# An attention layer on one core: attention and the first output quarter in the order of a list schedule, zero key halves from DRAM

## The chip, the core and the metric

The kernel runs on one core of a Trainium2 chip. The core has TensorE (PE) for matmuls, VectorE (DVE), ScalarE (ACT) and GpSimd (POOL) for elementwise work, and SyncE (SP), which issues most DMA transfers. Each engine takes its instructions from a queue of its own, in order, and waits on semaphores for what others must have done. The metric is device time in microseconds (us); lower is better. "Granted clock" is the share of TensorE's full clock that the profiler records.

## What is computed

One layer of a diffusion backbone on 512 latent tokens and 256 context tokens, width 2048, in float32. Both streams are normalised and modulated, projected, and go through two kinds of attention, eight heads of each, whose outputs are concatenated and projected by `w_o`. A gated MLP with a convolution follows. The part that the change touches, cut from the reference:

```python
def _diff_attend(q, k, v, lam):                       # 8 heads, two halves of 64 channels
    s1 = einsum('bhqd,bhkd->bhqk', q1, k1) * DA_SCALE
    s2 = einsum('bhqd,bhkd->bhqk', q2, k2) * DA_SCALE
    w = softmax(s1) - lam * softmax(s2)
    return einsum('bhqk,bhkd->bhqd', w, v)
def _softmax_attend(q, k, v, scale):                  # 8 latent heads, 128 + 64 channels
    return einsum('bhqk,bhkd->bhqd', softmax(einsum('bhqd,bhkd->bhqk', q, k) * scale), v)
o_da = _rmsnorm(o_da, subln_w) * (1.0 - lambda_init)  # per head
x = x + g1 * (concat(o_da, o_mla) @ w_o)
```

Queries are the 512 latent tokens, keys and values are all 768. Latent heads get queries, keys and values from small latents (`c_q`, `c_kv`) by a second projection; queries and keys of the latent tokens are rotated.

## The kernel before

A float32 product runs on TensorE as three matmuls of a faster 32-bit type: each operand is split into a high part (a cast, on ScalarE) and a low part (the rest, on VectorE), and `mm3` adds high by high, high by low and low by high. `split` and `wblock` make such pairs (lines 80, 81 and 104 to 106 in the profile); a weight block is a load `wr`, then `wh` and `wl`, with three buffers of each.

The stages around the change, in time:

- The projections of keys and values end with the values of heads 4 to 7: six tiles of PSUM are split into `kh` and `kl` (two buffers each) and stored to DRAM (`v_d`) by GpSimd.
- Eight differential heads (`da_head`). For each: the projection of the head's queries (`feature`, tile `f`, 16 steps of three matmuls), rotation and scaling into `qs`; keys `ks` (both parts stacked) and `klz` (low parts beside zeros) come from DRAM. For each quarter of 128 queries and each half: scores into a PSUM tile `s` of two buffers, a row maximum on VectorE, an exponential with its sum on ScalarE (line 514). GpSimd scales the second half (567), VectorE combines both (568). `weighted_values` then, for six blocks of 128 keys: four transposes into `pt`, a split into `wth` and `wtl`, and the product with the values into `po`. The output goes to DRAM (`o_d`).
- Eight latent heads, in pairs. `latent_pair` makes queries, keys and values of two heads; then scores of five matmuls, softmax, transposes, products. `sub_norm` normalises one differential head's output beside each latent head: a square, its sum over channels by a matmul with ones in plain float32 (653), four passes of VectorE.
- The output projection in four quarters of 64 steps of three matmuls each; the first three are in a loop (`for g in range(3)`), with passes over the modulation weights (`gemv`) from the second on.

The order of each engine's instructions comes from a scheduler that fills the queues by program order and priority; nothing is written by hand in this stretch. PSUM has, beside the two `s` buffers, four tiles here: one `pt`, two `f`, one `po`. The zero halves of `klz` and `krlz` are set by GpSimd with memsets.

```python
    for h in range(NH):
        da_head(h, da_queries(h))
    ap_.release()
...
        if i == 0 and h + 2 < NH:
            nxt = latent_pair(h // 2 + 1)
        sub_norm(h)
        oraw[8 + h] = b2k()
        weighted_values(mb, ws, lambda kt: [v[:, i * P:(i + 1) * P] for v in vs[kt]], oraw[8 + h], h == NH - 1)
```

Of the kernel before, what the change touches and what calls it, by code (L numbers as in the profile page):

```python
# [9 lines left out]
F32 = mybir.dt.float32  # L10
F32R = mybir.dt.float32r
# [37 lines left out]
NSMALL = _o  # L49


@with_exitstack
def layer_kernel(ctx: ExitStack, tc: tile.TileContext, small, rope, c_row, cc_row, x_t, ctx_t, ada, ada_k,
# [72 lines left out]
    ones32 = cst.tile([P, P], F32, name="ones32")  # L126
# [379 lines left out]
    def scores_softmax(mms, pool, tag, bufs, l):  # L506
        s = s_tile()
        for c0, c1 in ((0, T), (T, TT)):
            for i, (a, b) in enumerate(mms):
                pe.matmul(s[:, c0:c1], a, b[:, c0:c1], start=i == 0, stop=i == len(mms) - 1)  # L510
        m = sm.tile([P, 1], F32, tag="m", name=nm("m"), bufs=4)
        ve.tensor_reduce(out=m, in_=s[:, :TT], axis=AX.X, op=ALU.max, negate=True)
        p = pool.tile([P, TT], F32, tag=tag, name=nm(tag), bufs=bufs)
        sc.activation(p, s[:, :TT], AF.Exp, bias=m, accum_out=l)
        return p

    def weighted_values(pool, ws, v, dst, last=False):
        po = b_tile("po", 1)
        for kt in range(NKEY):
            pt = b_tile("f", 2) if last and kt % 3 else b_tile("pt", 1)  # L520
            for qt in range(NQT):
                pe.transpose(pt[:, qt * P:(qt + 1) * P], ws[qt][:, kt * P:(kt + 1) * P], ident)
            wth, wtl = split_tiles(pool, ("wth", "wtl"), [P, T], 2, pt)
            mm3(po, v(kt), (wth, wtl), kt == 0, kt == NKEY - 1)
        sc.copy(dst, po)
# [10 lines left out]
    def da_rtmp():  # L536
        return da.tile([P, T], F32, tag="rt", name=nm("rt"), bufs=2)

    def da_queries(h):
        if h == 0:  # L540
            qs = [da.tile([P, T], F32R, tag=f"qs{i}", name=nm("qs"), bufs=2) for i in range(2)]
            for i in range(2):
                nc.sync.dma_start(qs[i].bitcast(F32), q0_d[i])
            return qs
        lat = b_tile("f", 2)
        feature(lat, None)
        q = da_rtmp()
        apply_rope(q, lat, da_rtmp)
        return stacked_queries(da, q, DA_SCALE)

    def da_head(h, qs):
        ks = da.tile([P, 2, TT], F32R, tag="ks", name=nm("ks"), bufs=2)
        kl = klz[h % 2]
        for i, r in enumerate((lo, hi)):
            nc.sync.dma_start(ks[r].bitcast(F32), k_d[h][0].rearrange("(i p) n -> p i n", i=2))
            nc.sync.dma_start(kl[r, i].bitcast(F32), k_d[h][1][r])
        v = da.tile([P, 2, NKEY, P], F32R, tag="v", name=nm("v"), bufs=2)
        nc.sync.dma_start(v.bitcast(F32), v_d[h // 4][h % 4])
        ws = []
        for qt in range(NQT):  # L560
            c = slice(qt * P, (qt + 1) * P)
            l = sm.tile([P, 2], F32, tag="l", name=nm("l"), bufs=4)
            ps = [scores_softmax([(qs[i][:, c], ks[:, i]), (qs[i][:, c], kl[:, i])], da, f"p{i}", (8, 3)[i],
# [9 lines left out]

    for h in range(NH):
        da_head(h, da_queries(h))
    ap_.release()


    mc = tc.alloc_tile_pool(name="mc", bufs=1, side="right", reuse_waits="tile")
# [834 lines left out]
```

## Time and profile before

| | us |
|---|---|
| median of 3 runs (2439.32 to 2442.99) | 2439.42 |
| span of the profiled execution | 2439.6 |
| TensorE busy | 2367.0 |
| VectorE busy | 1735.5 |
| ScalarE busy | 1117.0 |
| GpSimd busy | 220.2 |

The profile is of one execution. A row of a timeline gives the start, the duration, the engine, the line, the operation and what it writes and reads; in brackets stands how long the engine sat idle before it and what ended that. A row of a group gives the count, the busy time and the mean in nanoseconds, then the idle time ahead of the group and its releasers. A wait row gives the total, the number of times and the longest. Where a shape is 128x512, a tile has 128 partitions and 512 elements in each.

### The profile page before, as it was taken

To read this page: it belongs to the slowest core of one execution; us is meant where nothing else is said; L and a number is where in the kernel's file an instruction comes from. 1 tells how busy PE (TensorE), PEld (TensorE's weight loads), DVE (VectorE), ACT (ScalarE), POOL (GpSimd) and SP (SyncE) were. 2 spreads that over 40 slices of the span, in tenths; PEclk is the share of its full clock that TensorE was granted. 3 is DMA by queue.
4 is the path that set the end of the run, shared out by engine and by line. 5 is a ranking of instruction groups with operands and counts; after the bars stand their busy time and mean duration, and the time that the engine had idled before them with its cause. 6 is when DMAs were issued, how large, how long until landed. Compare 5 with 4: busy or idle time off the path is not lost.

```text
span 2439.6 us, 32889 instructions
## 1 busy us (share of the span) xinstructions
PE 2367.0 (97%) x12758; PEld 1978.4 (81%) x12758; DVE 1735.5 (71%) x2316; ACT 1117.0 (46%) x1696; POOL 220.2 (9%) x244
## 2 busy tenths in 40 slices
PE   6999999999999999999999999999999999999998
PEld 3678877777777778889888888888888888888888
DVE  6668876388868878378667676767666666666667
ACT  4432121155646542245445454545454545454545
POOL 0000000121100003100111111111111111111110
PEclk9999999999999999999999999999999999999999
DMA  8758889555411149423555555555555565556573
GB/s 300 279 211 309 327 319 330 181 166 144 127 59 44 44 161 349 146 87 113 147 130 143 134 140 137 137 139 136 141 134 143 132 143 132 141 135 140 133 188 111
DMA packets 130707, 403.32 MB, mean 165 GB/s; under 512 B 14323, under 2 KB 25075, under 8 KB 122099
## 3 DMA queue, kind: packets, MB, share of 16 engines
q1 hardware_dynamic: 104118, 350.87, 43.7%
q0 software_dynamic: 25280, 49.30, 11.6%
q8 instruction: 100, 1.64, 0.3%
q10 hardware_dynamic: 1152, 1.05, 0.1%
q14 instruction: 57, 0.47, 0.1%
HBM read 331.68 MB, written 69.48 MB: 164 GB/s over the span
## 4 chain that ended last, share of the span: by engine, by line
PE 76%; DVE 8%; issue 7%; ACT 4%; DMA 3%; POOL 2%; SPq 0%; DVEq 0%; ACTq 0%; POOLq 0%
PE y L1133 11%; PE b L105 9%; PE b L104 9%; PE b L106 9%; PE z L1133 5%; PE y L1135 5%; PE s L104 3%; PE s L105 3%; PE s L106 3%; PE z L1135 3%; PE s L510 3%; PE x L1133 2%; DMA ada<-in_ada 2%; PE b L206 1%; PE f L104 1%
## 5 line engine op out<-in xcount | busy, mean ns | idle before, releaser
L989 DVE TENSOR_TENSOR wl<-wr,wh 128x1024 fp32r<-128x1024 f32 x144 | 176.4, 1225 | 157.8 <-ACT wh L981 157.1
L981 ACT CAST wh<-wr 128x1024 fp32r<-128x1024 f32 x144 | 151.0, 1049 | 234.0 <-PE b L105 118.5
L104 PE MATMUL b<-ah,wh 128*128 128x512 f32 (+1 forms) x664 | 256.8, 387 | 0.0
L105 PE MATMUL b<-al,wh 128*128 128x512 f32 (+1 forms) x664 | 256.7, 387 | 0.0
L106 PE MATMUL b<-ah,wl 128*128 128x512 f32 (+1 forms) x664 | 255.9, 385 | 0.0
L1154 POOL DMA_DIRECT2D x_d<-xs x160 | 139.6, 1004 | 1162.6 <-ACT xs L1153 1159.3
L989 DVE TENSOR_TENSOR wl<-rb,wh 128x1024 fp32r<-128x1024 f32 x123 | 150.0, 1220 | 126.9 <-ACT wh L981 126.8
L981 ACT CAST wh<-rb 128x1024 fp32r<-128x1024 f32 x123 | 129.2, 1050 | 185.7 <-PE b L105 116.1
L989 DVE TENSOR_TENSOR wl<-ws,wh 128x1024 fp32r<-128x1024 f32 x123 | 150.1, 1220 | 90.1 <-ACT wh L981 90.1
L80 ACT CAST wh<-wr 128x1024 fp32r<-128x1024 f32 (+3 forms) x102 | 99.2, 972 | 217.0 <-PE b L106 62.1
L171 DVE CUSTOM_DVE_ANT_0 ada<-ada,cb,smt 128x2048 f32<-128x2048 f32 x64 | 152.5, 2382 | 54.6 <-DMA ada<-in_ada 54.2
L981 ACT CAST wh<-ws 128x1024 fp32r<-128x1024 f32 x123 | 128.2, 1043 | 130.3 <-DVE ws L943 44.3
L1133 PE MATMUL y<-a2k,wh 128*128 128x512 f32 x656 | 164.0, 392 | 0.0
L81 DVE TENSOR_TENSOR wl<-wr,wh 128x1024 fp32r<-128x1024 f32 (+3 forms) x102 | 116.9, 1146 | 62.1 <-ACT wh L80 61.7
L104 PE MATMUL b<-a2k,wh 128*128 128x512 f32 (+1 forms) x376 | 141.6, 377 | 5.9 <-ACT a2k L838 4.3
L106 PEld LDWEIGHTS b<-ah,wl 128*128 128x128 f32 x664 | 124.8, 188 | 25.7
L104 PEld LDWEIGHTS b<-ah,wh 128*128 128x128 f32 x664 | 125.1, 188 | 22.9
L105 PEld LDWEIGHTS b<-al,wh 128*128 128x128 f32 x664 | 125.1, 188 | 21.9
L105 PE MATMUL b<-a2k,wh 128*128 128x512 f32 (+1 forms) x376 | 140.8, 374 | 0.0
L106 PE MATMUL b<-a2k,wl 128*128 128x512 f32 (+1 forms) x376 | 140.0, 372 | 0.0
L1133 PEld LDWEIGHTS y<-a2k,wh 128*128 128x128 f32 x656 | 118.6, 189 | 21.6
L1133 PE MATMUL y<-b2k,wh 128*128 128x512 f32 x410 | 107.8, 393 | 0.0
(454 smaller groups left out, 5757.2 us busy)
## 6 DMA issues: line engine op xcount, KB each, us to landing
ada<-in_ada SPq DMA_DIRECT2D x64, 1024.0 KB, 6.4
rb<-in_w_up SPq DMA_DIRECT2D x123, 512.0 KB, 4.3
wr<-in_w_dn SPq DMA_DIRECT2D x88, 512.0 KB, 4.3
x_d<-xs POOLq DMA_DIRECT2D x160, 256.0 KB, 6.0
wr<-in_w_up SPq DMA_DIRECT2D x53, 512.0 KB, 4.2
wr<-in_w_f SPq DMA_DIRECT2D x34, 512.0 KB, 6.0
ada<-in_ada SPq DMA_DIRECT2D x32, 512.0 KB, 6.4
adak<-in_ada_k SPq DMA_DIRECT2D x32, 512.0 KB, 6.3
```

Of the source, the lines that this page charges most:

```text
L80: sc.copy(dst_h, src)
L81: ve.tensor_tensor(dst_l, src, dst_h.bitcast(F32), op=ALU.subtract)
L104: pe.matmul(out, st[0], mv[0], start=start, stop=False, **kw)
L105: pe.matmul(out, st[0], mv[1], start=False, stop=False, **kw)
L106: pe.matmul(out, st[1], mv[0], start=False, stop=stop, **kw)
L171: ve.tensor_tensor_reduce(out=junk, in0=w, in1=vec, op0=ALU.mult, op1=ALU.add, scale=1.0, scalar=col("b_ada", j), accum_out=dst[:, j:j + 1])
L510: pe.matmul(s[:, c0:c1], a, b[:, c0:c1], start=i == 0, stop=i == len(mms) - 1)
L981: sc.copy(t, raw[:, k * n_:k * n_ + n_])
L989: ve.tensor_tensor(t, raw[:, k * n_:k * n_ + n_], hi[k].bitcast(F32), op=ALU.subtract)
L1133: pe.matmul(o, w[j][0], hs[j], start=start and j == 0, stop=False, skip_group_check=True)
L1135: pe.matmul(o[:, h0], w[j][1], hs[j][:, h0], start=False, stop=j == 7, skip_group_check=True)
L1154: gp.dma_start(x1_d[dt], x, accum_op=ALU.add)
```

## The change

Attention of both kinds and the first output quarter are no longer issued in the program's order. Each piece of work becomes a step with an engine, a cost, a due time `at`, and the buffers that it reads and writes. `Flow.run` goes through these steps as a list schedule: on each of five engines the open step with the least due time is taken, as far as its inputs are ready by the costs and a buffer of its ring is free. The instructions are then issued in that order, and the scheduler keeps it on all five engines. Due times come from a table of spans for the sixteen heads.

The work itself changes in these places:

- The zero halves of `klz` are loaded by SyncE from a block of zeros in DRAM, which GpSimd writes at the kernel's start from a zeroed tile. The latent heads' zero halves use the same tile.
- The combination of the two softmax maps: VectorE's pass over 768 columns is replaced by a scaling on ScalarE and a sum on GpSimd (behind GpSimd's scaling, which stays).
- `sub_norm`: the square is split in two parts, and its sum takes two matmuls of the faster type; VectorE's four passes and the final scaling go to GpSimd (six passes) and ScalarE.
- PSUM: two `pt`, one `f`, one `po`; four of a pair's six value blocks are projected into the unused columns of an `s` tile.
- Values of a latent pair share the buffers of the differential heads' values.
- The first output quarter's steps, and the splits of the sixteen head outputs that it reads, are in the same schedule; its gemv passes stay in the second and third quarters.

```diff
+class Flow:
+    LAGS = {"PE": 0.25, "ACT": 0.07, "DVE": 0.07, "POOL": 0.1, "SP": 3.5, "X": 0.0}
...
+            for e in engines:
+                while engines[e] <= now + 1e-9:
+                    can = [s for s in open_[e] if s.ready <= now + 1e-9 and all(free(b) for b in s.takes)]
+                    if not can:
+                        break
+                    s = min(can, key=lambda s: (s.at, s.n))
...
+                    engines[e] = now + s.cost
+                    order.append(s)
...
+        for s in order:
+            s.fn()
...
+    zero_d = dram.tile([64, TT], F32, name="zero_d")
...
+    for c0, c1, r in ((0, 480, slice(0, 64)), (480, TT, slice(64, P))):
+        gp.dma_start(zero_d[:, c0:c1].rearrange("p (k j) -> p k j", j=(c1 - c0) // KT),
+                     cpad[r, :, 2:2 + (c1 - c0) // KT])
...
-    def weighted_values(pool, ws, v, dst, last=False):
-        po = b_tile("po", 1)
+    def weighted_values(t, pace, ws, v, vr, dst, after=None):
+        po = buf(lambda: b_tile("po", 1), "po", 1)
         for kt in range(NKEY):
-            pt = b_tile("f", 2) if last and kt % 3 else b_tile("pt", 1)
...
+            pt = buf(lambda: b_tile("pt", 2), "pt", 2)
...
+            step("PE", 0.44, t0, turn, r=ws, w=[pt])
+            parts(t0 + 0.6, wt, pt, lambda b: b(), lambda pt=pt: pt())
+            step("PE", 0.69, t0 + 2.5, lambda wt=wt, kt=kt: mm3(po(), v(kt), [b() for b in wt], kt == 0,
+                                                                 kt == NKEY - 1), r=[*wt, *vr(kt)], w=[po])
...
+    SPANS = [17, 23.2, 23.2, 23.2, 23.2, 23.2, 23.2, 19] + [21, 22.8, 21, 22.8, 21, 22.8, 21, 16]
...
-    klz = [da.tile([P, 2, TT], F32R, name=nm("klz")) for _ in range(2)]
-    for t in klz:
-        for i, r in enumerate((hi, lo)):
-            gp.memset(t[r, i].bitcast(F32), 0.0)
+    for n_, (t, b) in enumerate(zip(klz, zeroed)):
+        for i, r in enumerate((hi, lo)):
+            step("SP", 0.1, FIRST + 3 * n_, lambda t=t, i=i, r=r: nc.sync.dma_start(t[r, i].bitcast(F32), zero_d), w=[b])
...
-            gp.tensor_scalar(out=ps[1], in0=ps[1], scalar1=rl[:, 1:2], scalar2=neglam, op0=ALU.mult, op1=ALU.mult)
-            ve.scalar_tensor_tensor(out=ps[0], in0=ps[0], scalar=rl[:, 0:1], in1=ps[1], op0=ALU.mult, op1=ALU.add)
+            step("POOL", 1.15, t + 0.2, lambda p=ps[1], rl=rl: gp.tensor_scalar(
+                out=p(), in0=p(), scalar1=rl()[:, 1:2], scalar2=neglam, op0=ALU.mult, op1=ALU.mult), r=[rl], w=[ps[1]])
+            step("ACT", 0.95, t + 0.2, lambda p=ps[0], rl=rl: sc.mul(p(), p(), rl()[:, 0:1]), r=[rl], w=[ps[0]])
+            step("POOL", 1.9, t + 1.5, lambda ps=ps: gp.tensor_tensor(out=ps[0](), in0=ps[0](), in1=ps[1](),
+                                                                      op=ALU.add), r=[ps[1]], w=[ps[0]])
...
-        pe.matmul(po, ones32, q, start=True, stop=True)
-        rstd(rs, po, P, mb.tile([P, T], F32, tag="sq", name=nm("s1"), bufs=1), t2)
+        step("ACT", 0.6, t + 4.4, lambda: sc.copy(qh(), q()), r=[q], w=[qh])
+        step("POOL", 1.3, t + 5, lambda: gp.tensor_tensor(out=ql(), in0=q(), in1=qh().bitcast(F32), op=ALU.subtract),
+             r=[q, qh], w=[ql])
+        step("PE", 0.46, t + 7, lambda: [pe.matmul(f(), onesr, g(), start=i == 0, stop=i == 1)
+                                         for i, g in enumerate((qh, ql))], r=[qh, ql], w=[f])
...
+    for kb in range(8):
+        t = tw + 8 * 0.9 * kb
+        w = block(t, w_o[0, kb])
...
+    with tc.manual_schedule(engines={mybir.EngineType.PE, mybir.EngineType.Activation, mybir.EngineType.DVE,
+                                     mybir.EngineType.SP, mybir.EngineType.Pool}):
+        flow.run()
```

**The start of the first differential head.** SyncE's queue before, behind the last value weights; `wr` are weight blocks of later query projections, `qs` and `ks` the first head's queries and keys:

```order
L90 DMA wr_3757<-in_w_f 128x1024
L90 DMA wr_4043<-in_w_f 128x1024
L90 DMA wr_4049<-in_w_f 128x1024
L90 DMA wr_4291<-in_w_f 128x1024
L90 DMA wr_4297<-in_w_f 128x1024
L543 DMA qs_3815<-q_d 128x512
L543 DMA qs_3816<-q_d 128x512
L555 DMA ks_3819<-k_d_128 64x2x768
```

The same place after:

```order
L215 DMA wr_3760<-in_w_f 128x1024
L755 DMA klz_3817<-zero_d 64x768
L765 DMA qs_3824<-q_d 128x512
L765 DMA qs_3826<-q_d 128x512
L755 DMA klz_3818<-zero_d 64x768
L755 DMA klz_3817<-zero_d 64x768
L755 DMA klz_3818<-zero_d 64x768
L773 DMA ks_3831<-k_d_128 64x2x768
```

Four weight blocks that stood ahead of the first queries and keys now stand behind them, and four loads of zeros are added. On VectorE, where `kl` are the low parts of the last values and `m` the row maxima of the scores, before:

```order
L81 TENSOR_TENSOR wl_4046<-wr_4043,wh_4045 128x1024
L81 TENSOR_TENSOR kl_3776<-s_3394,kh_3775 128x512
L81 TENSOR_TENSOR kl_3782<-s_3394,kh_3781 128x512
L81 TENSOR_TENSOR kl_3788<-b_3395,kh_3787 128x512
L81 TENSOR_TENSOR kl_3794<-b_3396,kh_3793 128x512
L81 TENSOR_TENSOR wl_4052<-wr_4049,wh_4051 128x1024
L512 TENSOR_REDUCE m_3832<-s_3827 128x1
```

and after:

```order
L206 TENSOR_TENSOR kl_3773<-s_3396,kh_3772 128x512
L206 TENSOR_TENSOR kl_3779<-s_3397,kh_3778 128x512
L206 TENSOR_TENSOR kl_3785<-s_3397,kh_3784 128x512
L206 TENSOR_TENSOR kl_3791<-b_3398,kh_3790 128x512
L206 TENSOR_TENSOR kl_3797<-b_3399,kh_3796 128x512
L698 TENSOR_REDUCE m_3859<-s_3851 128x1
L698 TENSOR_REDUCE m_3889<-s_3879 128x1
```

The splits of weight blocks between the value splits are gone from here; the value splits still stand ahead of the first maximum.

**The weights of a differential head.** TensorE before, where the second head's first transposes (`pt` from the weights `p` of its four quarters) stand among the third head's scores (`s`), the first head's last product (`po`) and a query projection (`f`):

```order
L106 MATMUL po_3919<-wth_3985,v_3824 128x512
L522 MATMUL pt_4168<-ident,p_4082 128x128
L522 MATMUL pt_4168<-ident,p_4105 128x128
L522 MATMUL pt_4168<-ident,p_4128 128x128
L510 MATMUL s_4346<-klz_3809,qs_4309 128x512
L510 MATMUL s_4346<-ks_4315,qs_4309 128x256
L510 MATMUL s_4346<-klz_3809,qs_4309 128x256
L104 MATMUL f_4490<-a2k_1556,wh_4299 128x512
L105 MATMUL f_4490<-a2k_1557,wh_4299 128x512
L106 MATMUL f_4490<-a2k_1556,wl_4300 128x512
L522 MATMUL pt_4168<-ident,p_4151 128x128
```

and after, at the third head's first transposes:

```order
L695 MATMUL s_4600<-ks_4272,qs_4506 128x512
L695 MATMUL s_4600<-klz_3818,qs_4506 128x512
L695 MATMUL s_4600<-ks_4272,qs_4506 128x256
L695 MATMUL s_4600<-klz_3818,qs_4506 128x256
L715 MATMUL pt_4607<-ident,p_4307 128x128
L715 MATMUL pt_4607<-ident,p_4346 128x128
L715 MATMUL pt_4607<-ident,p_4426 128x128
L715 MATMUL pt_4607<-ident,p_4512 128x128
L715 MATMUL pt_4614<-ident,p_4307 128x128
L715 MATMUL pt_4614<-ident,p_4346 128x128
L715 MATMUL pt_4614<-ident,p_4426 128x128
L715 MATMUL pt_4614<-ident,p_4512 128x128
```

The transposes of one block stand together, two blocks in a row, with the score's four matmuls in one piece ahead of them. On GpSimd, before:

```order
L498 DMA v_d_137<-kl_3794 128x4x128
L534 MEMSET klz_3809 64x768 x2
L534 MEMSET klz_3810 64x768 x2
L567 TENSOR_SCALAR p_3843<-p_3843,rl_3845,neglam 128x768
L567 TENSOR_SCALAR p_3866<-p_3866,rl_3868,neglam 128x768
```

and after:

```order
L628 DMA v_d_137<-kl_3797 128x4x128
L841 TENSOR_SCALAR p_3896<-p_3896,rl_3911,neglam 128x768
L844 TENSOR_TENSOR p_3869<-p_3869,p_3896 128x768
L841 TENSOR_SCALAR p_3937<-p_3937,rl_3952,neglam 128x768
L844 TENSOR_TENSOR p_3913<-p_3913,p_3937 128x768
```

The memsets behind the value stores are gone, and each scaling has a sum behind it.

More of the change, by code (lines that the diff above doesn't have):

```diff
@@ L125, in layer_kernel @@
     make_identity(nc, ident)
[L126 removed]
+    onesr = cst.tile([P, P], F32R, name="ones32")
+    ones32 = onesr.bitcast(F32)
     ve.memset(ones32, 1.0)
@@ L503, in layer_kernel @@
     ps_b = tc.alloc_tile_pool(name="ps_a", bufs=1, space=PSUM, reuse_waits="tile")
[L506 to L515, printed above, removed]
@@ L551, in da_head @@
[L551 to L558, printed above, removed]
+    flow = Flow()
+    step, buf = flow.step, flow.buf
@@ L691, in layer_kernel @@
     nc.sync.dma_start(cb, silu_c.to_broadcast([P, D]))
-    osp = []
-    for h in range(16):
-        hl = a2k(F32R), a2k(F32R, apb)
-        split(hl[0], hl[1], oraw[h])
-        osp.append(hl)
     def add_square(pool, ss, x, first):
```

558 lines of the change are left out of this document (435 added, 123 removed).

## The prediction

> **What bounds the kernel now.** I read the page first, then the windows over the attention, then TensorE's timeline for its pitches, then the waits. The page gives the frame, and the windows give the stretch that the change rewrites: from the first matmul of the first attention head's query projection to the first of the second output quarter.
>
> ```profile
> span 2439.6 us, 32889 instructions
> PE 2367.0 (97%) x12758; PEld 1978.4 (81%) x12758; DVE 1735.5 (71%) x2316; ACT 1117.0 (46%) x1696; POOL 220.2 (9%) x244
> ...
> 473.99:494.30 20.31, 15.54 (x60) 12.24 (x59) 7.57 (x10) 6.26 (x10) 10.52 (x15) 0.83 0.95 339
> 494.30:645.00 150.70, 147.75 (x738) 115.37 (x737) 132.02 (x192) 88.89 (x168) 30.93 (x26) 1.00 0.47 133
> 645.00:720.00 75.00, 66.50 (x351) 52.64 (x351) 59.85 (x100) 40.73 (x82) 8.08 (x8) 0.98 0.28 96
> 720.00:874.00 154.00, 146.75 (x790) 115.97 (x790) 122.75 (x215) 87.84 (x170) 0.00 (x0) 1.00 0.12 39
> 874.00:919.51 45.51, 45.51 (x208) 37.09 (x208) 32.65 (x38) 18.30 (x27) 1.39 (x3) 1.00 0.70 255
> ```
>
> The columns behind the length are the busy time and count of TensorE, its weight loads, VectorE, ScalarE and GpSimd, then the granted clock, the DMA share and GB/s. TensorE is the fullest engine in every row, but its busy time counts each matmul's latency, which overlaps the next; what it could do at best is read from the starts.
>
> ```profile
> 473.99 0.39 PE L104 MATMUL f<-a2k,wh 128*128 128x512 f32 x1
> ...
> 495.17 0.28 PE L510 MATMUL s<-ks,qs 128*128 128x256 f32 x1
> ...
> 495.40 0.40 PE L105 MATMUL f<-a2k,wh 128*128 128x512 f32 x1
> ...
> 875.27 0.60 PE L522 MATMUL pt<-ident,w 128*128 128x128 f32 x4
> 875.62 0.47 PE L104 MATMUL s<-a2k,wh 128*128 128x512 f32 x1
> 875.93 0.40 PE L105 MATMUL s<-a2k,wh 128*128 128x512 f32 x1
> 876.17 1.02 PE L653 MATMUL f<-sq,ones 128*128 128x512 f32 x2
> 877.03 0.60 PE L522 MATMUL f<-ident,w 128*128 128x128 f32 x4
> ...
> 886.19 0.39 PE L104 MATMUL s<-a2k,wh 128*128 128x512 f32 x1
> ...
> 919.28 0.39 PE L106 MATMUL s<-a2k,wl 128*128 128x512 f32 x1
> ```
>
> From 886.19 to 919.28 there are 146 steps of 128x512 without a gap: 0.2267 us each. The two narrow score matmuls at 495.17 take 0.115 each. Four transposes take 0.35, and the matmul behind them 0.31 in place of 0.227, so 0.43 together. The norm's sum (L653) in plain f32 takes 0.86.
>
> The code gives the counts in 473.99 to 919.51. 128x512: 336 for seven query projections, 288 for the products with the values, 128 and 160 for the scores of the two kinds of heads, 156 for the latent projections, 192 for the output quarter, together 1260, 285.6 us. 256 wide: 128, 160 and 192, 480 of them, 55.2. 96 groups of transposes, 41.3. Eight norms, 6.9. Sum 389.0 us of issue in 445.5, so **56.5 us in which TensorE could have worked and did not**. Added up along the timeline (start to start, less the pitch) the five stretches lose 7.5, 10.8, 17.0, 17.6 and 0.4; the other 3.2 lie mainly in transposes that were issued singly.
>
> Who is waited for:
>
> ```profile
> PEld pt L522 <- DVE p L568: 9.5, 11, 2.5
> ...
> PE s L510 <- DMA ks<-k_d: 4.6, 1, 4.6
> ...
> PEld po L104 <- ACT wth L80: 10.9, 31, 1.2
> ```
>
> The first two are from 472 to 700 us, the last from 700 to 940 (total, times, longest). In the differential heads transposes wait for the finished weights; at the start the scores wait for the keys; in the latent heads the product waits for the split of the transposes that stand right ahead of it.
>
> **The change, part by part.**
>
> *Matmul work.* The same matmuls but for the norm: sixteen steps of 0.2267 (3.6) for eight of 0.86 (6.9). New sum 385.7.
>
> *The start.* Before, the loads of queries and keys stand on SyncE's queue behind four weight blocks, and the zeroing of `klz` on GpSimd's behind the value stores. After, zeros, queries and keys stand ahead of the third weight block.
>
> ```profile
> 443.93 32.97 SPq L90 DMA_DIRECT2D wr<-in_w_f  x5
> 476.95 0.95 SPq L543 DMA_DIRECT2D qs<-q_d  x2
> ...
> 476.07 0.76 POOL L498 DMA_DIRECT2D v_d<-kh  x1 [0.48 <-ACT kh L80]
> ...
> 478.92 0.75 POOL L498 DMA_DIRECT2D v_d<-kl  x1
> ...
> 479.99 0.59 ACT L80 CAST kh<-b 128x512 fp32r<-128x512 f32 x1 [2.23 <-DMA v_d<-kh]
> ...
> 487.33 0.69 DVE L81 TENSOR_TENSOR kl<-b,kh 128x512 fp32r<-128x512 f32 x1 [2.50 <-DMA v_d<-kl]
> ```
>
> So the loads can go from about 444 instead of 477, and the wait of 4.6 us for keys goes. What is late next: the six last value splits. They stand ahead of the first row maximum on VectorE and of the first exponential on ScalarE before as after, and two `kh` buffers let them go only as fast as GpSimd's stores land: the last at 487.33, 8.4 us after the store of 478.92 that frees its buffer. That store ran beside the queries' and keys' loads, which now are long done; the store of 476.07 let ScalarE go at 479.99, 3.9 us. With 3.9 for the later ones the last split comes at about 482.8, ends at 483.5, and the first exponential (0.95 for the maximum, 1.1 for itself, rows below) at 485.6. In the new order TensorE does four projection steps, a score, three steps, a score, two steps (7.5 us) and then needs the score buffer that this exponential frees: it stands from 481.5 to 485.6. That is 4.1 us idle for 4.6.
>
> ```profile
> 484.40:489.00 4.60, 0.05 (x1) 0.08 (x1) 2.10 (x3) 1.53 (x2) 2.19 (x3) 0.82 1.05 360
> 489.00:494.30 5.30, 5.12 (x14) 3.90 (x15) 2.55 (x4) 2.01 (x4) 2.99 (x5) 0.51 1.01 393
> ```
>
> The idle time is followed by 5.3 us at half clock (0.51), some 2.7 us more, and I keep that too: the start keeps its 7.5. Bounds: 2 if the idle time is so short that the clock holds, 12 if the stores are as slow as before (488.0 in place of 483.5).
>
> *Zeros through DRAM.* Two stores of GpSimd put 196 KB into DRAM in the first microseconds, in pieces of 120 and 72 bytes, some 2,000 of them.
>
> ```profile
> 20.00:30.00 10.00, 1.12 (x2) 0.00 (x0) 9.59 (x15) 6.08 (x13) 0.00 (x0) 1.00 1.03 419
> 30.00:40.00 10.00, 6.55 (x40) 2.99 (x40) 6.69 (x10) 4.22 (x8) 0.00 (x0) 1.00 0.50 179
> ```
>
> From 20 to 30 us VectorE is the bound (9.59 of 10), and from 30 to 40 half of the DMA time is free: 5 us of cover on each DMA engine. I cost it at nothing; if the pieces take more than this cover, up to 2. The four loads of zeros fall into the value stage, where nothing waits for them. The later heads' keys wait on SyncE for the scores of the head before last to be done, and values and a weight block stand behind them; the order asks for these some 20 us of matmuls later, against 3.9 us for the transfer from 476.07 to 479.99, so I cost that at nothing; without this cover it would be a wait in each head.
>
> *The differential heads' weights.* VectorE's combining pass goes; ScalarE scales one half, and GpSimd adds after its own scaling. The rows that price this:
>
> ```profile
> L512 DVE TENSOR_REDUCE m<-s 128x1 f32<-128x768 f32 x52 | 48.8, 949 | 5.3 <-PE s L510 5.1
> L568 DVE SCALAR_TENSOR_TENSOR p<-p,rl,p 128x768 f32<-128x768 f32 x26 | 26.4, 1015 | 8.7 <-POOL p L567 8.2
> ...
> L81 DVE TENSOR_TENSOR wl<-wr,wh 128x1024 fp32r<-128x1024 f32 x10 | 12.1, 1215 | 0.0
> ...
> L514 ACT ACTIVATE p<-s,m 128x768 f32<-128x768 f32 x52 | 47.0, 904 | 35.5 <-DVE m L512 32.5 <-issue 1.7 <-ACT p L514 1.0
> ...
> L514 ACT ACTIVATION_READ_ACCUMULATOR p<-s,m 128x1 f32 x52 | 10.1, 195 | 0.0
> ...
> L567 POOL TENSOR_SCALAR p<-p,rl,neglam 128x768 f32<-128x768 f32 x32 | 37.5, 1173 | 146.3 <-DVE rl L566 141.3 <-ACT p L514 5.1
> L705 POOL TENSOR_TENSOR ss<-ss,sq 128x512 f32<-128x512 f32 x11 | 19.8, 1799 | 0.3
> ...
> L705 POOL TENSOR_TENSOR ss<-ss,sq x11: 1285/1729/2769, 919.3 to 1011.5; 128x512 f32<-128x512 f32 x11
> ...
> 965.98 1.30 POOL L705 TENSOR_TENSOR ss<-ss,sq 128x512 f32<-128x512 f32 x1
> ...
> 965.68 2.69 DVE L81 TENSOR_TENSOR wl<-wr,wh 128x1024 fp32r<-128x1024 f32 x1
> ```
>
> 52 maxima are six and a half heads. ScalarE: 88.9 us over 6.5 is 13.7 a head, and four scalings of about 0.90 make it 17.3. VectorE: 132.0 less 26.4 over 6.5 is 16.2. GpSimd: no 768-wide sum is in this trace; the 512-wide one takes 1.30 at best and 1.80 on average, by length 1.95 to 2.70, so a head costs four times 1.17 and 2.70, 15.5. TensorE needs 16 projection steps, 8 scores, 6 groups of transposes and 6 products: 23.1. It stays the bound, with the least room on ScalarE. The time from a head's last score to its finished weights is 0.95, 1.10, 1.17 and 2.70, about 6.3 us with the reciprocal and the hops (my allowance); the new order puts 7 to 11 us of other matmuls there, counted by their pitches, in every head but the seventh (3.4). So transposes, issued in fours now, hardly wait. I halve the 10.8 of these heads to **5** (bounds 0 and 10.8), and the 3.2 of single transposes to 1.
>
> *Hand-over, 645 to 720.* The first pair's latent projections now stand among the last head's scores. The seventh head misses 2.9 us; the eighth has no projection left, so ScalarE paces it, some 2.5 more: **5.5** of 17.0 (bounds 2 and 17).
>
> *Latent heads.* Two groups of transposes now stand ahead of the product, so its split has 1.4 us or more of other matmuls beside it; the norm's passes go to GpSimd, which did nothing here. I keep a third, **6** of 17.6 (bounds 0 and 13). The output quarter keeps its 0.4: its blocks are split during the last head, and the second quarter's gemv passes are queued behind the last splits.
>
> *Sum.* 385.7 and 7.5, 5, 5.5, 6, 0.4 and 1 make 411.1, which is 34.4 under 445.5. 2439.6 less 34.4 is 2405.2; the profiled execution is 0.2 over the median of the runs, so **2405**. Outside the stretch TensorE's order does not change.
>
> **The rivals.**
>
> *Everything hides.* Nothing but the start is left of the waits: 385.7 and 7.5 are 393.2, so 2387; with a short start 2381. For it: after 874 TensorE already runs 45 us without a gap. Against it: the eighth head lacks filling work.
>
> *GpSimd and VectorE block each other.* At 965.68 a pass of VectorE with two operands in SBUF takes 2.69 us, where its like takes 1.22 (L81), beside a GpSimd sum; and such sums take 1.29 to 2.77. A differential head has six such passes of VectorE; if each loses 1.47, VectorE needs 16.2 and 8.8, 25.0 us a head, 1.9 more than TensorE: 13 us over seven heads, 2418. The Trainium skill, "SBUF — State Buffer", section "Who interferes with whom", says that a VectorE instruction with two SBUF inputs and a GpSimd instruction that reads SBUF exclude each other for a whole instruction; the trace agrees, by 2.69 against 1.22. By that rule the passes moved to GpSimd cost VectorE part of what they free.
>
> *Slower: GpSimd becomes the differential heads' bound.* All of a head's sums stand on one queue and the transposes behind them. It decides when four scalings and four sums exceed 23.1 us by the 4.9 a head that the rest gains: a sum over 5.8 us. At 6.5 a head takes 30.7, seven heads lose 53, and the time is 2458. Against it: the longest 512-wide sum is 2.77, by length 4.2.
>
> *The waits only move.* The order is fixed by costs in the code; if they are off, the 53 us of waits come back elsewhere, and only the norm and the grouped transposes are won, some 5.5: 2434.
>
> **How the numbers follow.** A measurement of this kernel tells about 0.2% (5 us) from no change. Forecast (2393 to 2412) 0.54; everything hides (below 2393) 0.16; blocking (2412 to 2427) 0.18; waits move (2430 to 2444) 0.06, half of it within 0.2%; GpSimd's bound 0.06. Faster 0.90, same 0.04, slower 0.06. The range 2389 to 2427 takes in the forecast, the blocking and over half of the first rival: 0.8.
>
> **What would show it.** The stretch from the first `f` matmul to the first `b` matmul behind it near 411 us. The wait for `ks` gone, and one of about 4 us on the third score, released by the first exponential, with half clock behind it. Few waits of `pt` for the GpSimd sum. Sums of 768 near 2.7; `wl` passes of VectorE clearly over 1.22 would speak for the blocking. I am wrong if transposes wait for GpSimd in every head, or if the start costs over 12.

## The result, and the profile after

The changed kernel takes 2417.99 us (median of 4 runs, 2415.59 to 2421.25), the kernel before 2439.37 (2435.69 to 2442.99): a ratio of 0.9913, with a 95% interval of 0.9899 to 0.9927. The forecast was 2405. The page of the changed kernel:

```profile
span 2416.0 us, 33008 instructions
PE 2345.0 (97%) x12758; PEld 1980.2 (82%) x12758; DVE 1698.2 (70%) x2244; ACT 1154.3 (48%) x1752; POOL 334.8 (14%) x320
```

Its windows over the same stages, with the columns as before:

```profile
473.24:494.30 21.06, 18.88 (x88) 15.38 (x87) 12.75 (x18) 11.50 (x20) 13.01 (x14) 1.00 0.36 145
494.30:645.00 150.70, 143.21 (x723) 117.96 (x722) 113.77 (x165) 106.95 (x188) 71.65 (x49) 0.98 0.47 142
645.00:720.00 75.00, 70.64 (x398) 59.74 (x399) 61.32 (x99) 55.23 (x107) 30.48 (x23) 1.00 0.29 98
720.00:874.00 154.00, 149.40 (x839) 126.33 (x838) 114.15 (x184) 100.45 (x192) 43.29 (x36) 1.00 0.16 52
874.00:895.74 21.74, 21.74 (x97) 18.01 (x96) 14.23 (x13) 5.45 (x6) 1.39 (x3) 1.00 0.91 356
```

The start now runs at full clock (1.00, where it was 0.83). The stretch from the first `f` matmul to the first `b` matmul of the second output quarter goes from 473.24 to 895.74: 422.5 us in place of 445.5, that is 23.0 less, and 11.4 more than the forecast of 411.1. TensorE's timeline shows its ends and four of the five largest holes (the bracket is the idle time and what ended it; the fifth, of 1.67 us, stands before a score of the eighth head at 651.20):

```profile
473.24 0.39 PE L229 MATMUL f<-a2k,wh 128*128 128x512 f32 x1
...
483.13 0.50 PE L695 MATMUL s<-ks,qs 128*128 128x512 f32 x1 [2.18 <-ACT p L700]
...
558.14 1.12 PE L715 MATMUL pt<-ident,p 128*128 128x128 f32 x4 [3.19 <-DVE wtl L678]
...
584.83 0.76 PE L695 MATMUL s<-ks,qs 128*128 128x512 f32 x1 [1.91 <-ACT p L700]
...
853.18 0.50 PE L230 MATMUL po<-wtl,vh 128*128 128x512 f32 x1 [1.58 <-DVE wtl L678]
...
895.74 0.39 PE L229 MATMUL b<-a2k,wh 128*128 128x512 f32 x1
```

The holes that end at 558.14 and 584.83 stand behind a cast of a weight block on ScalarE. Among the waits from 473 to 660 us (total, times, longest) are these:

```profile
PEld s L695 <- ACT p L700: 13.2, 13, 2.6
PE s L695 <- ACT p L700: 9.3, 8, 2.2
ACT wh L658 <- DMA wr<-in_w_f: 8.1, 2, 4.4
PE pt L715 <- DVE wtl L678: 3.5, 2, 3.2
PEld pt L715 <- POOL p L844: 0.2, 1, 0.2
```

The transposes hardly wait for GpSimd's sums (0.2, once), as forecast. But ScalarE stands 8.1 us at two casts for the load of their block. In the timelines of SyncE's queue and of ScalarE, the first of the two:

```profile
540.88 0.61 SPq L773 DMA_DIRECT2D ks<-k_d  x1
...
544.18 0.33 SPq L784 DMA_DIRECT2D vh<-v_d  x1
...
545.75 2.51 SPq L646 DMA_DIRECT2D wr<-in_w_f  x2
...
548.95 0.89 ACT L700 ACTIVATE p<-s,m 128x768 f32<-128x768 f32 x1
...
554.32 1.05 ACT L658 CAST wh<-wr 128x1024 fp32r<-128x1024 f32 x1 [4.39 <-DMA wr<-in_w_f]
...
557.05 0.91 ACT L700 ACTIVATE p<-s,m 128x768 f32<-128x768 f32 x1
```

The load issued at 545.75 is waited for until 554.32: 8.57 us. `fetch` counts a `lag` of 4.0 for it. The block is due for the matmuls only some 10 us behind that cast's place (its cast is asked for 4 us ahead of its first use, its load 14), but the list schedule gives an engine without other work the first step that it believes to be ready, so the cast stands in ScalarE's order right where the data should have landed. Two exponentials, two splits of transposes and the scaling of a weight stand behind it, and TensorE soon needs all of them. The second hole is the same: a load issued at 575.75, its cast at 582.84.

To compare kernels, I added up for each head what TensorE lost from matmul start to matmul start, less the pitches of the forecast (0.2267 for 128x512 and so on), from each head's first score to the next head's. The eighth head's part ends with the first latent score; the latent heads' part holds the output quarter too. A profiled execution begins this stretch anywhere from 471.7 to 478.2, though the program ahead of it is all but the same (a large part of the difference arises at waits for value splits between 409 and 417 us, ahead of everything that the edits touch), and takes 1519.8 to 1521.6 behind it; so the length of the stretch tells small edits better than the total does. Stretch and stalls are of one execution each.

| kernel | stretch | start and first head | heads 2 to 7 | eighth | latent | median | ratio to before, 95% |
|---|---|---|---|---|---|---|---|
| changed kernel | 422.5 | 2.9 | 14.3 | 6.5 | 13.2 | 2417.99 | 0.9899 to 0.9927 |
| block counted at 8 us | 415.6 | 2.9 | 4.6 | 8.4 | 13.3 | 2413.63 | 0.9877 to 0.9907 |
| values 8 us later | 414.7 | 2.9 | 6.4 | 6.3 | 12.2 | 2415.57 | 0.9885 to 0.9914 |
| both | 416.9 | 4.4 | 4.2 | 8.4 | 13.1 | 2413.54 | 0.9874 to 0.9907 |
| blocks 6 us earlier | 414.1 | 6.8 | 3.0 | 6.4 | 11.4 | 2410.09 | 0.9862 to 0.9894 |
| combining on VectorE | 426.5 | 3.0 | 21.5 | 5.9 | 8.5 | 2421.86 | 0.9908 to 0.9941 |
| norm on VectorE | 424.7 | 4.4 | 11.6 | 7.6 | 14.1 | 2419.83 | 0.9905 to 0.9935 |
| zeros by GpSimd | 419.7 | 1.2 | 11.9 | 7.5 | 13.3 | 2415.07 | 0.9882 to 0.9911 |
| both, eighth head combined on VectorE | 416.8 | 3.4 | 4.1 | 9.7 | 12.8 | 2414.22 | 0.9874 to 0.9908 |
| both, other spans (a) | 409.9 | 5.0 | 3.4 | 7.9 | 7.2 | 2407.23 | 0.9843 to 0.9879 |
| both, other spans (b) | 407.3 | 4.9 | 4.9 | 4.7 | 5.8 | 2407.07 | 0.9844 to 0.9873 |

Three of these intervals lie clear of the changed kernel's, below it: blocks 6 us earlier and the two lists of other spans. For the other kernels the time alone tells no difference from the changed kernel, and the readings below rest on the stretch, the stalls and the waits.

### The profile page after: what moved, and what is told of

Its sections match the earlier page's. It is cut to its first block, busy times and chain, and to the rows that moved or that the text cites. A ratio compares the mean times of both kernels' runs of the same rounds, so it can differ in the third digit from the quotient of the medians.

```text
span 2416.0 us, 33008 instructions
## 1 busy us (share of the span) xinstructions
PE 2345.0 (97%) x12758; PEld 1980.2 (82%) x12758; DVE 1698.2 (70%) x2244; ACT 1154.3 (48%) x1752; POOL 334.8 (14%) x320
## 3 DMA queue, kind: packets, MB, share of 16 engines
q0 software_dynamic: 25376, 49.49, 11.6%
q10 hardware_dynamic: 1152, 1.05, 0.1%
## 4 chain that ended last, share of the span: by engine, by line
PE 70%; issue 16%; DVE 6%; ACT 3%; DMA 2%; POOL 2%; SPq 0%; DVEq 0%; POOLq 0%; ACTq 0%
PE b L230 8%; PE b L229 8%; PE b L231 8%; PE y L1537 8%; PE z L1537 4%; PE y L1539 4%; PE s L229 4%; PE s L231 4%; PE s L230 4%; PE s L695 3%; PE z L1539 2%; POOL x_d L1558 2%; PE x L1537 1%; PE pt L715 1%; PE f L229 1%
## 5 line engine op out<-in xcount | busy, mean ns | idle before, releaser
L205 ACT CAST wh<-wr 128x1024 fp32r<-128x1024 f32 (+1 forms) x69 | 67.5, 978 | 178.8 <-PE b L231 76.3
L1537 PEld LDWEIGHTS y<-a2k,wh 128*128 128x128 f32 x656 | 118.7, 189 | 21.5
L206 DVE TENSOR_TENSOR wl<-wr,wh 128x1024 fp32r<-128x1024 f32 (+1 forms) x69 | 80.1, 1161 | 52.5 <-ACT wh L205 52.0
L698 DVE TENSOR_REDUCE m<-s 128x1 f32<-128x768 f32 x96 | 90.9, 950 | 28.1 <-PE s L695 27.9
```

The costliest lines, as they stand in the source:

```text
L206: ve.tensor_tensor(dst_l, src, dst_h.bitcast(F32), op=ALU.subtract)
L698: step("DVE", 0.95, t + cost + 0.2, lambda: ve.tensor_reduce(out=m(), in_=s()[:, :TT], axis=AX.X, op=ALU.max, negate=True), r=[s], w=[m])
L1537: pe.matmul(o, w[j][0], hs[j], start=start and j == 0, stop=False, skip_group_check=True)
```

## The experiments

All are the changed kernel with one edit, or with the two edits to the loads and one more.

**A weight block counted at 8 us.**

```diff
-    def fetch(t, src, cols, lag=4.0):
+    def fetch(t, src, cols, lag=8.0):
```

> The list schedule is told that a weight block lands 8 us after its load instead of 4. Late-block theory (two of the differential heads' blocks land 8.55 and 7.07 us after their issue, ScalarE stands in order at their cast, and the exponentials queue behind it): the waits of the cast for the load (8.1 us in two places) go, the stalls from 494 to 645 fall from 15.9 to about 6, the half clock behind 554 and 582 goes, and the time falls by 8 to 10, to about 2409. Blocking theory (GpSimd and VectorE lengthen each other's passes): the order of the casts does not matter, 2418 within 3. ScalarE-bound theory (scores wait for exponentials because ScalarE has too much in these heads): 2418 within 3, with the stalls spread anew.

The casts' wait in this kernel, from 473 to 660 us:

```profile
ACT wh L658 <- DMA wr<-in_w_f: 0.5, 1, 0.5
```

The cast's waits go from 8.1 to 0.5, and the fourth and fifth heads' stalls from 10.7 to 0.8. The transfers are as slow as before (7.0 us in the median); only the order knows it. The stretch is 6.9 shorter, less than the 9.7 of heads 2 to 7, since the eighth head's stalls rise by 1.9 and its transposes stand apart more often, 0.8 more of pitch. Part of that rise is the clock: behind two holes of 2.15 and 2.38 us TensorE runs from 642.4 to 649.3 at a granted clock of 0.50, where the changed kernel keeps 1.00. The median falls by 4.4, not by the 8 to 10 expected. The late-block theory holds for the waits and the stalls that it named; by the other two the casts' place would not have mattered.

**The values' loads 8 us later.**

```diff
-        load_values(b + 2, h)
+        load_values(b + 10, h)
```

> The loads of a differential head's values (768 KB) are asked for 8 us later, behind the weight block instead of ahead of it; the schedule still counts 4 us for a block. Late-block theory, if the burst of keys, values, an output and two blocks (3.3 MB) is what makes the block late: the block lands about 2 to 3 us sooner, the two waits of ScalarE fall from 8.1 to about 3 together, and the time falls by 4 to 6, to about 2413. If the block is late for another reason (its own 512 KB take 7 us in any company): no change, 2418 within 3. Blocking theory: no change.

The same place in SyncE's and ScalarE's timelines of this kernel:

```profile
550.47 1.33 SPq L646 DMA_DIRECT2D wr<-in_w_f  x1
551.89 0.38 SPq L784 DMA_DIRECT2D vh<-v_d  x1
...
555.88 1.05 ACT L658 CAST wh<-wr 128x1024 fp32r<-128x1024 f32 x1 [0.98 <-DMA wr<-in_w_f]
```

And of its waits from 473 to 660 us:

```profile
ACT wh L658 <- DMA wr<-in_w_f: 2.1, 2, 1.1
```

With 768 KB of values behind it and not ahead of it, the block is there 5.4 us after its issue, 3.2 sooner. The planner still counts 4, so the cast waits 0.98 where it waited 4.39. At the second place the block takes 7.0 us, as good as before (7.1), but it is issued earlier: counted from the first load of keys, the two blocks are there after 10.0 and 9.9 us, where it was 13.4 and 12.4. So the block is late because of what stands ahead of it on the queue. The stretch is 7.9 shorter. The median is only 2.4 lower, which the expectation for no change (2418 within 3) also allows; what speaks for the theory is the block and its cast.

**Both.** The two edits together.

> Both edits to the loads together: 8 us counted for a block, and the values' loads 8 us later. Late-block theory: each edit alone already took most of the stalls of the fourth and fifth heads (10.7 us to 0.8 and to 2.6), so together they take no more than the first: 0.4 a head, a stretch of 414 to 416 us against 422.5, and 2412 to 2414. If the loads held back something else besides the casts, the gains (6.9 and 7.9 us of the stretch) add to more than 10: a stretch below 412.

Heads 2 to 7 keep 4.2 of stalls, against 4.6 with the first edit alone: the two edits take away the same wait, as expected. The stretch of 416.9 is a little over the 414 to 416 expected: the start loses 4.4 in place of 2.9, by the clock (last section).

**Blocks 6 us earlier.**

```diff
-        step("SP", 0.1 * len(src), t - 14, load, w=[raw], lag=lag)
+        step("SP", 0.1 * len(src), t - 20, load, w=[raw], lag=lag)
```

> The loads of the weight blocks are asked for 6 us sooner (20 us ahead of their use instead of 14), still with 4 us counted for each. Late-block theory: one block of each head then goes ahead of the burst of keys and values, the other follows it; the planner puts the casts as early as it believes the data to be there, so a cast can still stand ahead of a late block: stalls of the fourth and fifth heads anywhere from 1 to 11 us, but each one found behind a cast that waits for its load. If the distance from load to use were what matters, and not the planner's 4 us: no waits of casts for loads, 0.4 a head.

No wait of a cast for a load is left in its profile from 473 to 660 us, and heads 2 to 7 keep 3.0. I had left open whether casts would still stand ahead of late blocks; none does, and 3.0 over six heads is near the 0.4 a head of the second reading. So the distance from a load to its cast is what matters, and the planner's 4 us only as far as they set it: no cast stands less than 6 us behind its load here. The edit shifts the first head's order as well, whose stalls rise from 2.9 to 6.8. Its interval of the ratio (0.9862 to 0.9894) lies below that of the changed kernel.

**The combining pass back on VectorE.**

```diff
-            step("ACT", 0.95, t + 0.2, lambda p=ps[0], rl=rl: sc.mul(p(), p(), rl()[:, 0:1]), r=[rl], w=[ps[0]])
-            step("POOL", 1.9, t + 1.5, lambda ps=ps: gp.tensor_tensor(out=ps[0](), in0=ps[0](), in1=ps[1](),
-                                                                      op=ALU.add), r=[ps[1]], w=[ps[0]])
+            step("DVE", 1.02, t + 1.5, lambda ps=ps, rl=rl: ve.scalar_tensor_tensor(
+                out=ps[0](), in0=ps[0](), scalar=rl()[:, 0:1], in1=ps[1](), op0=ALU.mult, op1=ALU.add),
+                 r=[ps[1], rl], w=[ps[0]])
```

> The combination of a differential head's two weights goes back to one pass of VectorE, 24 of 768 wide at about 1.02 us; ScalarE's scaling (0.94) and GpSimd's sum (1.90) go. Blocking theory: VectorE takes 4.1 us a head more in place of the 1.0 a head that its passes now lose beside the sums; it has 5.7 us a head to spare, so 2418 within 4, slower if anything. ScalarE-bound theory: ScalarE is relieved of 3.7 us a head of 16.4, the 22 us of waits of scores for exponentials fall by half, and the time falls by 5 or more. Late-block theory: the casts stay where they are, so most of the 15.9 us of stalls stay; 2418 within 5.

Waits of this kernel, 475 to 665 us:

```profile
PEld s L695 <- ACT p L700: 19.1, 13, 4.2
...
ACT wh L658 <- DMA wr<-in_w_f: 13.5, 3, 7.2
```

It is no faster, though ScalarE has 3.7 us a head less to do; the scores wait longer for exponentials, not shorter. That ScalarE's load is not what bounds these heads is told better by the first experiment: there ScalarE scales as much as in the changed kernel, and heads 2 to 7 lose 4.6. Between the blocking and the late-block theory this run does not decide; 2421.86 suits both. What the edit itself costs is not told by this run: the new order puts three casts ahead of late blocks (13.5 us of waits in place of 8.1), which may alone make the difference of 4.0 in the stretch. And the latent heads, whose code the edit leaves alone, lose 8.5 in place of 13.2: each edit shifts the whole order behind it.

**The norm's passes on VectorE.** All six POOL steps of `sub_norm` become VectorE steps, three of them shown:

```diff
-        step("POOL", 1.1, t + 10, lambda: gp.tensor_tensor(out=t2(), in0=rs(), in1=rs(), op=ALU.mult), r=[rs], w=[t2])
+        step("DVE", 0.7, t + 10, lambda: ve.tensor_tensor(out=t2(), in0=rs(), in1=rs(), op=ALU.mult), r=[rs], w=[t2])
...
-        step("POOL", 1.4, t + 13, lambda: gp.tensor_tensor(out=rs(), in0=rs(), in1=t2(), op=ALU.mult), r=[t2], w=[rs])
-        step("POOL", 1.4, t + 14, lambda: gp.tensor_tensor(out=o(), in0=o(), in1=rs(), op=ALU.mult), r=[rs], w=[o])
+        step("DVE", 0.7, t + 13, lambda: ve.tensor_tensor(out=rs(), in0=rs(), in1=t2(), op=ALU.mult), r=[t2], w=[rs])
+        step("DVE", 0.7, t + 14, lambda: ve.tensor_tensor(out=o(), in0=o(), in1=rs(), op=ALU.mult), r=[rs], w=[o])
```

> The six passes of a head's norm go from GpSimd to VectorE (about 3.9 us a head in place of 7 on GpSimd). Blocking theory: in the latent heads VectorE's passes with two operands in SBUF are lengthened only beside these (the low parts for the output projection took 1.36 in place of 0.68 at 848 us, and the product at 853 stood 1.58 us for them); without GpSimd this goes, the stalls from 720 to 874 fall from 10.6 by 3 to 5, and the time falls by as much, to about 2414. VectorE-bound theory: 31 us more of work on VectorE, which is busy 114 of 154 us there, lengthens its queue by more than the blocking did; the stalls rise by 3 to 10 and the time goes to 2421 to 2428.

The changed kernel first (VectorE and GpSimd at one time), then this one:

```profile
848.45 4.08 DVE L1078 TENSOR_TENSOR a2k<-or,a2k 128x512 fp32r<-128x512 f32 x3
...
848.49 1.79 POOL L972 TENSOR_TENSOR sr<-sr,s 128x512 f32<-128x512 f32 x1
```

```profile
850.98 0.68 DVE L1078 TENSOR_TENSOR a2k<-or,a2k 128x512 fp32r<-128x512 f32 x1
```

The blocking is real: three low parts take 4.08 us beside GpSimd, 1.36 each, and 0.68 each without it; the hole of 1.58 at 853 goes. But the latent heads lose 14.1 in place of 13.2, for other waits take its place, and the stretch is 2.2 longer, 1.5 of it at the start, which the edit does not touch. So blocking made single holes, and moving the work off GpSimd gives nothing back. The result lies between the two theories' numbers.

**The zeros by GpSimd again.**

```diff
-            step("SP", 0.1, FIRST + 3 * n_, lambda t=t, i=i, r=r: nc.sync.dma_start(t[r, i].bitcast(F32), zero_d), w=[b])
+            step("POOL", 0.73, FIRST + 3 * n_, lambda t=t, i=i, r=r: gp.memset(t[r, i].bitcast(F32), 0.0), w=[b])
```

> The zero halves of the low keys are set by GpSimd again, as before, behind its value stores; all else as in the changed kernel. If the zeros from DRAM are what takes away the wait for keys (4.6 us before): the four memsets (0.73 each) come after 482, the first head's low keys are loaded behind them, and the start's stalls rise from 2.9 by 6 to 12 (that wait, some 3 us of load and half clock behind it), to a stretch of 429 to 435. If only the order of SyncE's queue mattered: 422.5 within 2.

This kernel's timelines of GpSimd and TensorE at the start:

```profile
485.08 3.10 POOL L755 MEMSET klz<- 64x768 f32 x4
...
486.25 0.39 PE L695 MATMUL s<-ks,qs 128*128 128x512 f32 x1
```

I was wrong here in both theories. The memsets do come late (485.08), but the loads of the keys do not wait for them (they write other halves), and the planner, which knows of the memsets, puts 45 of the 48 projection matmuls ahead of the first score, at 486.25. By then the value splits are done too: the start loses 1.2 in place of 2.9. Four casts wait for late blocks here (12.6 us), but spread as some 2 us of stalls in each of heads 2 to 6, 10.9 together against 13.4 in the changed kernel. The zeros from DRAM gain nothing here; the wait for keys went with the memsets in place too. That it went because the list schedule has the keys loaded early and can fill in is my reading; no run parts the two.

**The eighth head combined on VectorE.** Both edits to the loads, and the combining edit above for `h == NH - 1` alone.

> The two edits to the loads, and the combination on VectorE in the eighth differential head alone, which takes 3.7 us from ScalarE and puts 4.1 on VectorE there. If ScalarE paces the eighth head: its stalls (6.5 us in the changed kernel, 6 to 8 with the edits to the loads) fall by 3 or more, to a stretch of 411 to 412. If the turn of the two score buffers paces it (maximum, exponential and release one behind the other), or work that lies ready for TensorE is missing: the stalls stay at 6 to 8, a stretch of 414 to 416.

The eighth head loses 9.7 in place of 8.4: taking work from ScalarE and giving it to VectorE does not help, so nothing speaks for ScalarE's load as what paces this head. But VectorE, which makes the maxima, has 4.1 us more to do there, and that could hide a gain. The turn of the score buffers and missing work remain; this run does not part them.

**Other due times.** Both edits to the loads, with new lists of spans; in the second, blocks are also loaded 13 us ahead and not 14:

```diff
-    SPANS = [17, 23.2, 23.2, 23.2, 23.2, 23.2, 23.2, 19] + [21, 22.8, 21, 22.8, 21, 22.8, 21, 16]
+    SPANS = [13.5, 23.2, 23.0, 23.2, 22.4, 23.2, 25.2, 18.3] + [21.6, 22.8, 22.5, 25.1, 22.5, 24.5, 17.2, 14.5]
```

```diff
-    SPANS = [17, 23.2, 23.2, 23.2, 23.2, 23.2, 23.2, 19] + [21, 22.8, 21, 22.8, 21, 22.8, 21, 16]
+    SPANS = [13.3, 23.5, 21.8, 22.8, 20.1, 24.2, 25.6, 18.3] + [21.6, 23.3, 22.3, 26.1, 21.7, 25.0, 17.0, 13.5]
```

> The two edits to the loads and other due times of the heads (the list of spans), chosen so that by the kernel's own planning costs TensorE is left without work for a third to a half less than with the old spans. With the loads mended, the hand-over (8.4 us) and the latent heads (13.1) hold most of the 30.2 us of stalls. If these stalls lie in the schedule itself (the planner sees them too and the chip only follows): they fall by 6 to 10 us, to a stretch of 407 to 411 and a time of 2404 to 2408. If they come from what the planner does not know (GpSimd and VectorE lengthening each other's passes, late transfers): they stay, 415 to 418 and 2411 to 2415.

> A second set of spans of the same kind, with weight blocks asked for 13 us ahead of their use instead of 14; by the planning costs it leaves TensorE 1.4 us less without work than the first. If the stalls lie in the schedule itself: a stretch of 405 to 411, within 3 of the first set. If the planner does not see them: 415 to 418.

The ends of the stretch in the second one's timeline:

```profile
476.68 0.39 PE L229 MATMUL f<-a2k,wh 128*128 128x512 f32 x1
...
883.97 0.39 PE L229 MATMUL b<-a2k,wh 128*128 128x512 f32 x1
```

The stretches are 409.9 and 407.3, and the times 2407.23 and 2407.07: within the expectation for stalls that lie in the schedule itself. The latent heads' stalls fall from 13.1 (both edits to the loads) to 7.2 and 5.8, with the norm still on GpSimd. The second kernel, at a ratio of 0.9859 (0.9844 to 0.9873) to the kernel before, beats the changed kernel (0.9913); the two kernels with other spans are level with each other and have the lowest times of all.

## Why the prediction was right or wrong

The sign and the range were right; the forecast of 2405 was 13 us too low. The range held 2418 because it took in the blocking, which is not what came about, so that part was luck. Its terms against the table: start 7.5 against 2.9, heads 2 to 7 5 against 14.3, hand-over 5.5 against 6.5, latent heads 6 against 13.2, output quarter 0.4 against 0, singles 1 (contained in the others now). With the work, 385.7 against 385.6, the difference adds up: -4.6, +9.3, +1.0, +7.2, -0.4, -1.0 and -0.1 are +11.4. The forecast cut the stretch at times and the table cuts it at heads; cut at the forecast's times, the changed kernel loses some 3, 15, 8, 11 and 0 us, so the hand-over was further off than the table makes it and the latent heads nearer.

*Matmul work.* Right, and so is the norm by two matmuls.

*The start: over-sized.* The chain was the forecast one: value splits held by GpSimd's stores, then the maximum, the exponential, the third score. The mis-sized step is the 3.9 us from a store to the split that it frees. In the changed kernel's timelines of GpSimd and VectorE:

```profile
477.84 0.75 POOL L628 DMA_DIRECT2D v_d<-kl  x1 [0.23 <-DVE kl L206]
...
480.50 0.69 DVE L206 TENSOR_TENSOR kl<-b,kh 128x512 fp32r<-128x512 f32 x1 [1.01 <-DMA v_d<-kl]
```

It is 2.7. So the last split ends at 481.2 and not at 483.5, TensorE stands 2.2 us and not 4.1, and the clock holds, which saves the other 2.7. That it held was luck in part: with both edits to the loads, and with the norm on VectorE, the hole is as long (2.18 and 2.17 us), half clock follows, and the start loses 4.4.

*Zeros at nothing: a cost that was there.* The cover was looked for from 20 to 40 us, but the two stores are issued at 1.7 and 2.8 and land 8.9 and 11.4 us later, while the first inputs are loaded. Windows from 10 to 20 us (the last two columns are DMA share and GB/s) and TensorE's next matmuls, first of the kernel before, then of the changed one:

```profile
10.00:20.00 10.00, 10.00 (x13) 3.81 (x12) 7.72 (x11) 6.83 (x14) 0.00 (x0) 1.00 1.06 406
...
31.50 2.93 PE L306 MATMUL s<-sqs,ones 128*128 128x512 f32 x4 [10.38 <-DVE sqs L299]
```

```profile
10.00:20.00 10.00, 10.00 (x13) 3.66 (x11) 5.47 (x7) 5.19 (x10) 0.00 (x0) 1.00 0.98 259
...
34.06 2.93 PE L436 MATMUL s<-sqs,ones 128*128 128x512 f32 x4 [13.13 <-DVE sqs L429]
```

The DMA engines are about as full and move 259 GB/s in place of 406, VectorE gets its inputs later, and TensorE goes on 2.6 us later; in the ten other kernels, which all keep these stores, it is 2.5 to 3.3. No run leaves the stores out, so the cause is read from the timing alone. The total does not show it: the kernel before stands at half clock from 415.6 to 419.1 us, the changed one does not, and so its stretch still begins 0.8 us earlier. That the wait for keys would go was right; with memsets in place of the four loads it goes as well.

*"The later heads' keys wait on SyncE ... so I cost that at nothing": the step that failed most.* It set one transfer of 3.9 us against some 20 us of matmuls ahead of the use. Both sides were the wrong ones. The block's load stands behind 1.15 MB of keys, 768 KB of values and a 256 KB output, and takes 8.57 us and not 3.9. And the first in need of it is not TensorE but ScalarE, at a cast that the planner had set 4 us behind the load. These two heads lost 10.7 us, and 0.8 once the planner counted 8 us for a block; the other four lost 3.6, so the 5 for the weights was about right.

*The differential heads' weights.* Right in kind: groups from 494 to 645 us.

```profile
L844 POOL TENSOR_TENSOR p<-p,p 128x768 f32<-128x768 f32 x24 | 45.5, 1896 | 22.7 <-issue 16.8 <-POOL p L841 4.1 <-ACT p L843 1.4
...
L659 DVE TENSOR_TENSOR wl<-wr,wh 128x1024 fp32r<-128x1024 f32 x11 | 16.4, 1491 | 8.2 <-ACT wh L658 8.0
L803 DVE SCALAR_TENSOR_TENSOR qs<-rt,qs 64x512 fp32r<-64x512 f32 x14 | 11.9, 852 | 0.4
L795 DVE TENSOR_TENSOR rt<-rt,ropet 128x512 f32<-128x512 f32 x6 | 5.5, 913 | 0.1
```

GpSimd's sum takes 1.90 and not 2.70, just under the lower of my bounds (1.95). GpSimd as the bound is far off.

*Blocking.* The rival's time of 2418 is what came out, but by another way. At their lengths alone (1.22, 0.69 and 0.68) the three kinds of VectorE passes would take 6.6 us less over six and a half heads, 1.0 a head, where the rival said 8.8. I had let every such pass meet a sum in full; most do not. The Trainium skill, "SBUF — State Buffer", section "Who interferes with whom", holds for those that do, as in the changed kernel's timelines here:

```profile
569.51 2.05 POOL L844 TENSOR_TENSOR p<-p,p 128x768 f32<-128x768 f32 x1 [0.19 <-POOL p L841]
...
569.88 2.77 DVE L659 TENSOR_TENSOR wl<-wr,wh 128x1024 fp32r<-128x1024 f32 x1
```

*Hand-over and latent heads.* The 5.5 was near the eighth head's 6.5 (some 8 from 645 to 720), but for its reason, ScalarE pacing the eighth head, nothing spoke in the run that relieved ScalarE there. The third that I kept for the latent heads was a guess without a row: 6 against 13.2. Other due times took about half of these stalls, so these lay in the order, which I had read only at three places.

## What to carry to other kernels

A list schedule turns each wrong lag into a fixed place in an in-order queue: an idle engine gets the step just where the planner believes its data to be, and the late data then holds up everything behind it. Price a load by all that is issued ahead of it, and find the first instruction in any queue that needs it, not the matmul that uses it last. Price a transfer in small pieces also by what it does to the loads beside it. When the order is worked out by a planner, compare stalls head by head, for an edit in one place moves the order in all that follow.

## What the runs showed of the hardware

*A burst of loads fills the DMA engines at half their best rate.* The changed kernel's windows over the burst (the last three columns are granted clock, DMA share and GB/s):

```profile
544.00:546.00 2.00, 2.00 (x11) 1.71 (x10) 1.97 (x3) 1.42 (x3) 0.00 (x0) 1.00 1.05 217
...
550.00:552.00 2.00, 2.00 (x12) 1.71 (x11) 0.99 (x2) 0.00 (x0) 1.93 (x2) 1.00 1.05 414
```

Both are full (1.05), at 217 and at 414 GB/s. Why the first part is slower was not tried.

*The clock fell after a shorter idle time than one it stood through.* Windows of the changed kernel behind its holes that end at 558.14, 584.83 and 483.13:

```profile
558.10:561.20 3.10, 3.06 (x10) 2.63 (x11) 0.75 (x3) 1.46 (x4) 1.17 (x2) 0.53 0.00 0
...
584.60:588.00 3.40, 2.86 (x9) 2.38 (x10) 3.40 (x6) 2.86 (x7) 1.78 (x1) 0.54 0.00 0
...
483.10:487.00 3.90, 3.87 (x19) 3.31 (x20) 2.30 (x4) 2.63 (x5) 0.68 (x1) 1.00 0.11 44
```

An idle time of 2.18 us left the clock at 1.00; 3.19 and 1.91 brought it to 0.53 and 0.54 for about 3 us. In the kernel with both edits to the loads, the same hole of 2.18 us did bring it down, to 0.50:

```profile
483.00 0.80 PE L695 MATMUL s<-ks,qs 128*128 128x512 f32 x1 [2.18 <-ACT p L700]
...
482.75:486.17 3.42, 3.17 (x9) 2.59 (x10) 1.52 (x4) 2.43 (x6) 0.33 (x1) 0.50 0.18 75
```

So length alone does not decide. The Trainium skill, "TensorE: Matmul & The Clock Gate", section "What's actually happening", tells of a free-running window of about 3.4 us, which fits that, but puts the half clock behind at least one idle window; the 1.91 us here is shorter than one.
